# A product-key expert layer on one core: the split of the expert scores between streamed and gathered columns, 1536 and 512 against 1408 and 640

## The chip, the cores and the metric

The kernel runs on one core of one Trainium2 chip. The metric is the device time of one execution, in microseconds (us). The shown time is the median of 3 runs. One more execution was taken by the hardware profiler; its span is the time from its first to its last instruction.

## The reference, cut to what matters

A decoder layer for 256 tokens of 2048 values: a mixer (projections, two convolutions, a recurrence) and then a product-key expert layer. The change is in the expert layer:

```python
q = (hf @ wq).reshape(t, 8, 2, 128)                      # 8 heads, two halves
scores = einsum('thpd,hpnd->thpn', q, subkeys)           # 128 keys per half
# top 16 of each half, then the top 16 of their sums: 16 experts a head and token
expert_idx = row * 128 + col                             # of 16384 experts
act = einsum('cd,chkd->chk', hb, take(u_table, expert_idx))  # the expert scores
w = gates * gelu(act)
y = einsum('chk,chkd->cd', w, take(v_table, expert_idx))
```

Each token needs 128 scores: the products of its 2048 values with the 2048 values of 128 rows of the u table.

## The kernel before, in words

The stages follow one another: modulation and mixer (to about 475 us of the span), queries, top-k and expert scores (about 475 to 1138 us, the stage of the change), the weighting of the chosen experts (about 1138 to 1318 us), the v table and the output.

**The score of one expert is made in two parts.** The first `DU` = 1536 of the 2048 values are streamed: for each of 128 rows of 128 experts (`urows`, 64 to 127 and then 0 to 63) the block `ud[r]` is loaded and multiplied with all 256 tokens on TensorE, and the result goes to row r of the large tile S (L815). The last `GU` = 512 values are gathered: for each of the 256 pairs of a token half (128 tokens, one in each partition) and a chosen slot, GpSimd issues an indirect DMA that brings one row of `ug` per partition (L726), and VectorE forms the product with the tokens' values, which lie in PSUM as `h2n`, and sums it into `actg` (L732, called a dot here). The next stage adds the two parts.

**A streamed row is worked in pieces.** `UPARTS` cuts the `KU` = 12 slices of 128 values into two pieces of 6. `piece` loads its part (L785), splits it on ScalarE into a high part (L95) and on VectorE into a low part (L96, called a sub here), and issues 3 matmuls of 128x256 for each slice (L788, L790 for the high part, L792 for the low one). High and low parts have rings of two buffers each, so a piece can't be split before the piece two ahead of it has left TensorE. The query columns (`wq`, 16 slices in `QPARTS` of 6, 6 and 4) go through the same `piece`; head 0 computes four columns, for heads 0 and 1, head 1 none, each later head two. Four PSUM accumulators (`paccB`) are there beside two banks for `h2n` and one for `misc`.

**The order on VectorE is written out by a planner at build time.** The stage stands in a `manual_schedule` of VectorE. After each piece `room` calls `fill`, which keeps two ledgers in nanoseconds. `clock[1]` is VectorE's free time: each piece adds 327 per slice less the price of its sub, and each top-k step and dot issued takes its price off (`dve(n)` = 69 + n/0.96). `clock[2]` is the DMA's free time: each piece adds 327 per slice less 182 for its own load, capped at the price of one gather, and a gather (`GU`*512/360: 728) is issued while it is above 0, a buffer is free and a chosen slot is known. A dot may come `LAG` = 3 pieces behind its gather. Head h+1 begins after 16 pieces (`NU`); what is left of older top-k work then is issued at once (`finish`).

**The buffers of the gathers** are 6 in the tile R (`guS`) and 30 that are lent from rows of S that aren't written yet (`lend`, rows 12 to 46 and 102 to 128, `UG` = 2 rows each). `retire` takes them back before S is written there, so that in the last 32 streamed rows only those in R are left. R is also where the next stage keeps its transposed indices (`trs`, L882 to L892) and its first two broadcast rows (`rawR`, L949).

**The end of the stage** is this loop; nothing else follows it on VectorE before the next stage:

```python
        while dots or units:
            clock[2] = 1e9
            gathers()
            dot()
```

The next stage (L949 to L999) builds one-hot matrices from `cold` (SyncE load, ScalarE L951 and L952), forms scores in PSUM (L959), picks with VectorE (L965, `choose`), and builds weights with GpSimd (L988, `sides`), VectorE (L993) and TensorE (L995). Its PSUM tiles lie where `h2n` and the accumulators were.

Of the kernel before, what the change touches and what calls it, by code (L numbers as in the profile page):

```python
# [16 lines left out]
AF = mybir.ActivationFunctionType  # L17
# [4 lines left out]
T = 256  # L22
D = 2048
KT = D // 128
# [13 lines left out]
LAG = 3  # L38
DOTS = 3
SLACK = 0  # L40
UG = 2
EG = 2
COLR = 48
BURST = 1
# [2 lines left out]
QPARTS = ((0, 6), (6, 12), (12, 16))  # L47
# [15 lines left out]
XUF = 4  # L63
# [2 lines left out]
MSTEP = (1, 0)  # L66
NFIRST = 10
NACC = 5
DU = 1536
KU = DU // 128  # L70
GU = D - DU
KSL = (6, 6, 4)
DV = 1536
GV = D - DV
UPARTS = ((0, 6), (6, 12))

PCOLS = {}
_n = 0
# [9 lines left out]
def build(nc, tc, A, stop=None):  # L88
# [5 lines left out]
    def split(h, l, src, eng=None):  # L94
        nc.scalar.activation(h, src, AF.Copy)  # L95
        (eng or nc.vector).tensor_tensor(l, src, h, op=OP.subtract)  # L96
# [143 lines left out]
    accum = lambda: pacc.tile([128, T], F32, name="acc")  # L240
# [147 lines left out]
    for j in range(4):  # L388
        n = 0
# [224 lines left out]
    Sf = S.rearrange("p b t r -> p (b t r)")  # L614
# [3 lines left out]

    def flat(a, n):

        return Sf[:, a * T:(a + n) * T]

    def rows(a, n):
        return flat(a, n).rearrange("p (a b) -> p a b", b=T)


    UW = UPARTS[0][1]
    ua = Area(0, RKB - 9)
# [11 lines left out]
    ufR = Area(RKB - 9, RKB).ring(3, UW * 128)  # L640
    guS = [ua.t(GU) for _ in range(int((ua.end - ua.at) // GU))]
    sub = kc(flat(0, 8))
    qring = Ring([rows(8, 2), rows(10, 2)])
    nc.sync.dma_start(sub, A["sub"])
# [105 lines left out]
    def lend(at):  # L750
        lent[at] = flat(at, UG)[:, :GU]
        free.append(lent[at])
# [21 lines left out]
    def finish():  # L774
        for t in tops.pop(0)[1]:
            clock[1] -= t
        gathers()

    def piece(ps, src, k0, k1, end, late=False):

        n = (k1 - k0) * 128
        w = kc(ufR()[:, :n])
        uh, ul = uHr(), uLr()
        with tc.high_priority(offset=HP):
            nc.sync.dma_start(w, src[:, k0:k1, :])  # L785
            split(uh[:, :k1 - k0], ul[:, :k1 - k0], w)
        for k in range(k0, k1):
            nc.tensor.matmul(ps, uh[:, k - k0, :], hH(k), start=k == 0, stop=False)  # L788
            if not late:
                nc.tensor.matmul(ps, uh[:, k - k0, :], hL(k), start=False, stop=False)  # L790
        for k in range(k0, k1):
            nc.tensor.matmul(ps, ul[:, k - k0, :], hH(k), start=False, stop=k == end - 1)  # L792
        for k in range(k0, k1 if late else k0):
            nc.tensor.matmul(ps, uh[:, k - k0, :], hL(k), start=False, stop=False)

    def room(k0, k1):
        n = (k1 - k0) * 128
        fill((k1 - k0) * 327 - dve(n) + SLACK, n * 512 / 360, (k1 - k0) * 327)
# [4 lines left out]
    def upiece():  # L803
        if "parts" not in state or not state["parts"]:
            state["r"] = r = urows.pop(0)
            state["parts"] = list(UPARTS)
            state["ps"] = accum()
# [7 lines left out]
            nc.scalar.activation(srow(r), ps, AF.Copy)  # L815
        room(k0, k1)

    for at in list(range(12, 60 - 3 * XUF - UG, UG)) + list(range(102, 129 - UG, UG)):
        lend(at)
    more = [flat(60 - 3 * i - 3, 3) for i in range(XUF)]  # L820
    with tc.manual_schedule(engines={mybir.EngineType.DVE}):
        for h in range(NH):
            if h != 1:
                n = 4 if h == 0 else 2
                cols = [accum() for _ in range(n)]
                for k0, k1 in QPARTS:
                    for a in range(n):
                        piece(cols[a], A["wq"][2 * h + a], k0, k1, KT, h == 0 and k0 == 0)
                        room(k0, k1)
                qss = [qring() for _ in range(n // 2)]  # L830
                for a in range(n):
                    nc.scalar.activation(qss[a // 2][:, a % 2, :], cols[a], AF.Copy)
            qs = qss.pop(0)
            if h == 0:
                nc.scalar.activation(tab, qs[:, 0, :1], AF.Exp, scale=0.0)
            if h == 0:
                ufR.aps = ufR.aps + more
            for tt in range(2):
                ps = misc()
                for a in range(2):  # L840
                    nc.tensor.matmul(ps[:, 128 * a:128 * a + 128], qs[:, a, tt * 128:tt * 128 + 128],
                                     sub[:, 2 * h + a, :], start=True, stop=True)
                while len(tops) >= 2:
                    finish()
                sc = scR()
                nc.scalar.activation(sc, ps[:, :256].rearrange("p (a b) -> p a b", a=2), AF.Copy)
                tops.append((clock[0], topk(h, tt, sc)))
            for _ in range(NU):
                upiece()
        while tops:  # L850
            upiece()
# [91 lines left out]
    at = lambda g: (g * TG // NK, g * TG % NK)  # L943
# [223 lines left out]
def arrays(i):  # L1167
# [5 lines left out]
    def slabs(w):  # L1173
# [12 lines left out]
        "sub": c_(i["peer_subkeys"][0].reshape(2 * NH, NK, 128).transpose(2, 0, 1)),  # L1186
        "ud": c_(i["peer_u"][0][:, :DU].reshape(NK, NK, KU, 128).transpose(0, 3, 2, 1)),
        "ug": c_(i["peer_u"][0][:, DU:]),
        "vd": c_(i["peer_v"][0][:, :DV].reshape(NK, NK, DV)),
# [13 lines left out]
```

## Time and profile before

| | us |
|---|---|
| median of 3 runs | 1884.22 (1877.45 to 1885.96) |
| the profiled execution, its own time | 1884.01 |
| span of the profiled execution | 1882.0 |
| busy in the span: TensorE matmul | 1795.1 (95%) |
| VectorE | 1523.8 (81%) |
| ScalarE | 958.5 (51%) |
| GpSimd | 786.7 (42%) |
| DMA moved | 530.03 MB, mean 282 GB/s |

In the profile PE is TensorE (PEld its weight loads), DVE is VectorE, ACT is ScalarE, POOL is GpSimd, SP is SyncE. L726 is line 726 of the kernel. `out<-in` are the program's tile names with their digits left out. A busy share is a mean over stages with different limits; what counts is which engine had no gap in the stage in question. Matmuls overlap in the records: one lasts 0.28 us there, while a new one starts every 0.12 us.

### The profile page before, as it was taken

What the parts mean: (1) busy time and instruction counts of PE and PEld (TensorE: products, weight loads), DVE (VectorE), ACT (ScalarE), POOL (GpSimd) and SP (SyncE); (2) the same over time, 40 slices, a digit from 0 to 9 for tenths busy, and PEclk for the clock granted to TensorE, in tenths of its full rate; (3) what the DMA queues carried; (4) which work ended last, traced back from release to release, by engine and by line L of the source; (5) the groups of instructions that cost most, each with busy time, mean ns of one, the idle gap of its engine ahead of it and who ended that gap; (6) DMA issues with size and microseconds to landing.
All of it is one profiled execution on the core that took longest, in us unless ns stands there. A gap on an engine that the chain in (4) does not pass through costs nothing.

```text
span 1882.0 us, 34335 instructions
## 1 busy us (share of the span) xinstructions
PE 1795.1 (95%) x11978; PEld 1544.5 (82%) x11978; DVE 1523.8 (81%) x3946; ACT 958.5 (51%) x1474; POOL 786.7 (42%) x789
## 2 busy tenths in 40 slices
PE   6999999999899999999999998998999999999996
PEld 2667777787899999999999997887777787778774
DVE  3349998755789999999877777999788888888887
ACT  3243333743665555555555558884444444544443
POOL 0000000000035555324555635997776566666662
PEclk8999999999999999999999999999999999999998
DMA  8998889796779989878999886552799889898884
GB/s 311 372 358 277 295 301 322 254 332 249 258 248 302 297 298 300 277 248 288 306 306 305 283 294 200 177 146 80 276 317 335 322 318 313 310 313 313 311 299 155
DMA packets 174652, 530.03 MB, mean 282 GB/s; under 512 B 20736, under 2 KB 44304, under 8 KB 167056
## 3 DMA queue, kind: packets, MB, share of 16 engines
q1 hardware_dynamic: 132656, 391.50, 61.9%
q0 software_dynamic: 40960, 134.25, 19.9%
q8 instruction: 94, 1.54, 0.3%
q10 hardware_dynamic: 864, 2.10, 0.3%
q14 instruction: 78, 0.64, 0.1%
HBM read 521.40 MB, written 6.37 MB: 280 GB/s over the span
## 4 chain that ended last, share of the span: by engine, by line
PE 51%; issue 15%; POOL 14%; DVE 10%; DMA 9%; ACT 2%; SPq 0%; POOLq 0%; ACTq 0%; DVEq 0%
PE acc L788 11%; PE acc L790 11%; PE acc L792 11%; POOL S L1065 7%; DMA PF<-in_w_in_dram 4%; PE acc L354 3%; PE acc L355 3%; PE acc L357 3%; POOL sh L988 3%; PE modps L279 2%; DMA R<-in_vd_dram 2%; POOL sl L1065 2%; POOL sh L1065 2%; PE acc L365 1%; DVE PF L435 1%
## 5 line engine op out<-in xcount | busy, mean ns | idle before, releaser
L788 PE MATMUL acc<-sh,sb 128*128 128x256 f32 x1792 | 443.1, 284 | 1.0 <-ACT sb L95 0.5
L790 PE MATMUL acc<-sl,sb 128*128 128x256 f32 x1768 | 438.9, 284 | 0.4 <-DVE sl L563 0.4
L788 PEld LDWEIGHTS acc<-sh,sb 128*128 128x128 f32 x1792 | 342.6, 192 | 3.4 <-ACT sh L557 2.2
L790 PEld LDWEIGHTS acc<-sl,sb 128*128 128x128 f32 x1768 | 339.3, 192 | 0.6 <-DVE sl L563 0.6
L95 ACT ACTIVATE sb<-R 128x768 fp32r<-128x768 f32 (+2 forms) x203 | 197.1, 971 | 230.0 <-PE acc L790 113.1
L96 DVE TENSOR_TENSOR sb<-S,sb 128x768 fp32r<-128x768 f32 (+3 forms) x274 | 219.0, 800 | 97.0 <-ACT sb L95 84.0
L726 POOL DMA_INDIRECT R<-in_ug_dram,ei x119 | 130.7, 1099 | 386.2 <-ACT gt L705 253.3
L95 ACT ACTIVATE sb<-S 128x768 fp32r<-128x768 f32 (+3 forms) x274 | 207.3, 758 | 115.3 <-PE acc L790 89.4
L792 PE MATMUL acc<-sh,sb 128*128 128x256 f32 x1792 | 264.8, 283 | 0.0
L1065 POOL DMA_INDIRECT S<-in_vg_dram,ei x158 | 214.7, 1359 | 115.6 <-DVE R L1074 84.5
L792 PEld LDWEIGHTS acc<-sh,sb 128*128 128x128 f32 x1792 | 237.1, 192 | 0.0
L1092 PE MATMUL o<-sl,sb 128*128 128x512 f32 x900 | 222.5, 394 | 12.1 <-DVE sl L96 9.4
L1092 PE MATMUL o<-sh,sb 128*128 128x512 f32 x888 | 218.4, 394 | 11.5 <-DVE sh L96 10.2
L726 POOL DMA_INDIRECT S<-in_ug_dram,ei x137 | 153.4, 1120 | 167.4 <-DVE ei L714 97.1
L1092 PEld LDWEIGHTS o<-sl,sb 128*128 128x128 f32 x900 | 166.4, 188 | 57.2 <-DVE sl L96 18.9
L1092 PEld LDWEIGHTS o<-sh,sb 128*128 128x128 f32 x888 | 166.2, 189 | 54.0 <-DVE sh L96 17.8
L96 DVE TENSOR_TENSOR sb<-R,sb 128x768 fp32r<-128x768 f32 (+1 forms) x160 | 150.1, 938 | 51.9 <-ACT sb L95 40.2
L988 POOL TENSOR_SCALAR sh<-iot,R 128x128 f32<-128x128 f32 x248 | 144.8, 602 | 35.3 <-ACT R L892 21.1
L1092 PE MATMUL o<-sb 128*128 128x512 f32 x516 | 126.3, 390 | 0.5 <-ACT sb L95 0.5
L1074 DVE SCALAR_TENSOR_TENSOR R<-S,R 128x512 f32<-128x512 f32 x157 | 117.5, 748 | 3.5 <-DMA S<-in_vg_dram,ei 0.7
L95 ACT ACTIVATE PR<-PF 128x1024 fp32r<-128x1024 f32 (+2 forms) x81 | 66.2, 826 | 95.7 <-DMA PF<-in_w_in_dram 57.5
L1092 PEld LDWEIGHTS o<-sb 128*128 128x128 f32 x516 | 96.7, 188 | 21.2 <-ACT sb L95 0.9
(291 smaller groups left out, 3331.7 us busy)
## 6 DMA issues: line engine op xcount, KB each, us to landing
R<-in_vd_dram SPq DMA_DIRECT2D x128, 768.0 KB
PF<-in_w_mod_dram SPq DMA_DIRECT2D x86, 1024.0 KB
R<-in_ud_dram SPq DMA_DIRECT2D x132, 384.0 KB
S<-in_ud_dram SPq DMA_DIRECT2D x124, 384.0 KB
PF<-in_w_in_dram SPq DMA_DIRECT2D x44, 512.0 KB
PF<-in_w_out_dram SPq DMA_DIRECT2D x32, 512.0 KB
PF<-in_w_in_dram SPq DMA_DIRECT2D x40, 256.0 KB
sl<-in_w_mod_dram SPq DMA_DIRECT2D x20, 512.0 KB
```

The costliest lines, as they stand in the source:

```text
L95: nc.scalar.activation(h, src, AF.Copy)
L96: (eng or nc.vector).tensor_tensor(l, src, h, op=OP.subtract)
L354: nc.tensor.matmul(ps, h[:, k - k0, :], rh(k), start=first and k == k0, stop=False)
L355: nc.tensor.matmul(ps, h[:, k - k0, :], rl(k), start=False, stop=False)
L726: nc.gpsimd.indirect_dma_start(out=g, out_offset=None, in_=A["ug"], in_offset=bass.IndirectOffsetOnAxis(ap=ei[:, tt, s_:s_ + 1], axis=0))
L788: nc.tensor.matmul(ps, uh[:, k - k0, :], hH(k), start=k == 0, stop=False)
L790: nc.tensor.matmul(ps, uh[:, k - k0, :], hL(k), start=False, stop=False)
L792: nc.tensor.matmul(ps, ul[:, k - k0, :], hH(k), start=False, stop=k == end - 1)
L988: eng.tensor_scalar(Bt[:, i, :], iot, trs[tt][:, 1, b + i:b + i + 1], None, op0=OP.is_equal)
L1065: nc.gpsimd.indirect_dma_start(out=g, out_offset=None, in_=A["vg"], in_offset=bass.IndirectOffsetOnAxis(ap=ei[:, tt, s_:s_ + 1], axis=0))
L1074: nc.vector.scalar_tensor_tensor(og[:, tt, :], g, wn[:, tt, s_:s_ + 1], og[:, tt, :], op0=OP.mult, op1=OP.add)
L1092: nc.tensor.matmul(out[tt][n], a[:, tt * 128:tt * 128 + 128], b[:, 512 * n:512 * n + 512], start=r == 0 and a is wh and b is vh, stop=r == ...
```

## The change

The streamed part has 1408 values (11 slices, in pieces of 6 and 5) and the gathered part 640. The lent buffers take 2.5 rows of S each, so that 14 and 10 of them fit where 17 and 13 did, and R holds 5 buffers of 640 values where it held 6 of 512. `h2n` takes two banks for each token half, four in all, and three accumulators are left; for these, every head computes its own two query columns, head 0 and head 1 too. The host cuts the u table accordingly.

```diff
-UG = 2
+UG = 2.5
-DU = 1536
+DU = 1408
-UPARTS = ((0, 6), (6, 12))
+UPARTS = ((0, 6), (6, 11))
@@ flat
-        return Sf[:, a * T:(a + n) * T]
+        return Sf[:, int(a * T):int((a + n) * T)]
@@
-    for at in list(range(12, 60 - 3 * XUF - UG, UG)) + list(range(102, 129 - UG, UG)):
-        lend(at)
+    for a, b in ((12, 60 - 3 * XUF), (102, 128)):
+        for i in range(int((b - a) / UG)):
+            lend(a + i * UG)
@@ for h in range(NH)
-            if h != 1:
-                n = 4 if h == 0 else 2
-                cols = [accum() for _ in range(n)]
-                for k0, k1 in QPARTS:
-                    for a in range(n):
-                        piece(cols[a], A["wq"][2 * h + a], k0, k1, KT, h == 0 and k0 == 0)
-                        room(k0, k1)
-                qss = [qring() for _ in range(n // 2)]
-                for a in range(n):
-                    nc.scalar.activation(qss[a // 2][:, a % 2, :], cols[a], AF.Copy)
-            qs = qss.pop(0)
+            cols = [accum() for _ in range(2)]
+            for k0, k1 in QPARTS:
+                for a in range(2):
+                    piece(cols[a], A["wq"][2 * h + a], k0, k1, KT, h == 0 and k0 == 0)
+                    room(k0, k1)
+            qs = qring()
+            for a in range(2):
+                nc.scalar.activation(qs[:, a, :], cols[a], AF.Copy)
```

`KU`, `GU`, the number of PSUM banks of `h2n` (`HB`), of accumulators (`5 - HB`) and of buffers in R follow from these by the lines of before.

## Rows read from the trace of the kernel before

**Rows 1.** Page: busy us (share of the span) and instructions of each engine.

```profile
PE 1795.1 (95%) x11978; PEld 1544.5 (82%) x11978; DVE 1523.8 (81%) x3946; ACT 958.5 (51%) x1474; POOL 786.7 (42%) x789
```

**Rows 2.** Stretches: from:to length, busy us (instructions) by engine, PEclk, DMA share, GB/s.

```profile
538.00:880.00 342.00, 341.51 (x2827) 339.14 (x2826) 319.25 (x1329) 196.63 (x401) 153.52 (x140) 1.00 0.88 287
880.00:1060.00 180.00, 180.00 (x1503) 180.00 (x1502) 143.30 (x324) 94.12 (x125) 96.28 (x84) 1.00 0.90 296
...
1138.00:1318.00 180.00, 166.03 (x1273) 140.55 (x1272) 164.11 (x822) 131.42 (x231) 149.72 (x252) 0.98 0.51 151
```

**Rows 3.** TensorE at the stage's start, in order of time: start us, duration us, what.

```profile
488.70 0.39 PE L790 MATMUL acc<-sl,sb 128*128 128x256 f32 x1 [0.39 <-DVE sl L563]
...
505.43 0.61 PE L841 MATMUL misc<-S 128*128 128x128 f32 x4
```

**Rows 4.** VectorE at the same place, in order of time: the last low part.

```profile
493.27 0.69 DVE L563 TENSOR_TENSOR sl<-PF,sh 128x512 fp32r<-128x512 f32 x1 [0.36 <-ACT sh L557]
```

**Rows 5.** Source line 726, the gathers: ns min/median/max, first and last start us.

```profile
L726 POOL DMA_INDIRECT S<-in_ug_dram,ei x137: 940/947/1693, 548.2 to 983.9; - x137
L726 POOL DMA_INDIRECT R<-in_ug_dram,ei x119: 940/947/1692, 534.8 to 1118.3; - x119
```

**Rows 6.** Groups by line and shape from 560 to 1240: the subs of two sizes.

```profile
L96 DVE TENSOR_TENSOR sb<-R,sb 128x768 fp32r<-128x768 f32 x131 | 125.2, 955 | 39.5 <-ACT sb L95 31.3 <-issue 7.0 <-ACT R L846 0.8
...
L96 DVE TENSOR_TENSOR sb<-S,sb 128x512 fp32r<-128x512 f32 x6 | 4.2, 695 | 0.3 <-ACT sb L95 0.3
```

**Rows 7.** VectorE in order of time: two dots, one behind the other.

```profile
705.79 0.68 DVE L732 SCALAR_TENSOR_TENSOR R<-S,h2n 128x512 bf16<-128x512 f32 x1
...
706.51 0.69 DVE L732 SCALAR_TENSOR_TENSOR R<-S,h2n 128x512 bf16<-128x512 f32 x1
```

**Rows 8.** Sub, dot and gather in the last streamed rows, in order of time.

```profile
1097.04 0.96 DVE L96 TENSOR_TENSOR sb<-R,sb 128x768 fp32r<-128x768 f32 x1 [0.60 <-ACT sb L95]
...
1097.92 0.68 DVE L732 SCALAR_TENSOR_TENSOR R<-R,h2n 128x512 bf16<-128x512 f32 x1
...
1098.88 0.94 POOL L726 DMA_INDIRECT R<-in_ug_dram,ei  x1 [1.22 <-DVE R L732]
```

**Rows 9.** GpSimd in order of time: two gathers in a row; one during a sub.

```profile
542.10 0.94 POOL L726 DMA_INDIRECT R<-in_ug_dram,ei  x1 [1.57 <-DVE ei L714]
543.34 0.94 POOL L726 DMA_INDIRECT R<-in_ug_dram,ei  x1 [0.30 <-issue]
...
1027.92 0.96 DVE L96 TENSOR_TENSOR sb<-R,sb 128x768 fp32r<-128x768 f32 x1 [0.53 <-issue]
...
1028.31 1.38 POOL L726 DMA_INDIRECT R<-in_ug_dram,ei  x1 [0.30 <-issue]
```

**Rows 10.** The v table's gathers: issue on GpSimd, use on VectorE, two pairs.

```profile
1321.35 1.34 POOL L1065 DMA_INDIRECT sh<-in_vg_dram,ei  x1 [9.81 <-DVE R L1072]
1323.00 2.15 POOL L1065 DMA_INDIRECT sh<-in_vg_dram,ei  x1 [0.31 <-DVE R L1074]
...
1325.60 0.75 DVE L1074 SCALAR_TENSOR_TENSOR R<-sh,R 128x512 f32<-128x512 f32 x1
1329.34 0.75 DVE L1074 SCALAR_TENSOR_TENSOR R<-sh,R 128x512 f32<-128x512 f32 x1 [2.99 <-DMA sh<-in_vg_dram,ei]
```

**Rows 11.** The stage's end, in order of time, VectorE and TensorE.

```profile
1133.76 0.96 DVE L96 TENSOR_TENSOR sb<-R,sb 128x768 fp32r<-128x768 f32 x1 [1.20 <-ACT sb L95]
1137.00 0.88 PE L792 MATMUL acc<-sh,sb 128*128 128x256 f32 x6
...
1140.27 0.35 DVE L965 SCALAR_TENSOR_TENSOR R<-iot,R,G 128x128 bf16<-128x128 f32 x1 [5.55 <-ACT R L892]
1147.60 0.35 DVE L965 SCALAR_TENSOR_TENSOR R<-iot,R,G 128x128 bf16<-128x128 f32 x1 [4.17 <-PE G L959]
1153.42 0.98 PE L995 MATMUL W<-sl,sh 128*128 128x128 f32 x4 [0.80 <-DVE sl L993]
```

**Rows 12.** The chain that ended last, in order of time: start us, us, what.

```profile
1131.41 5.13 DMA R<-cold
```

## The prediction

> **What bounds the kernel now.** I read the page's engine shares first, then the stretches of the stage, then the instructions at its two ends in order of time. The shares put TensorE at 95% [rows 1], which says little about one stage; the stretches say more. From 538 to 1060 us TensorE has no gap (341.51 of 342, 180.00 of 180) [rows 2]; the reader should see that 1503 matmuls in 180 us are one every 0.120 us, and 180/1503 = 0.1198 is the price used below. VectorE is close behind where the top-k work runs (319 of 342, 93%) and loose later (143 of 180); the DMA engines stand at 0.90 with 296 GB/s [rows 2]. So TensorE bounds this stage, with VectorE and the DMA near. In the stage behind it VectorE (164 of 180) and GpSimd (150 of 180) set the pace [rows 2], and TensorE has room.
>
> **The change part by part.**
>
> *The removed slice.* 128 streamed rows lose 3 matmuls each: 384 x 0.1198 = 46.0 us less on the bounding engine. This has one answer as long as nothing else becomes late.
>
> *Two query columns first instead of four.* Before, the four columns give TensorE 4 x 16 x 3 x 0.1198 = 23.0 us of work while the normed tokens are still being made; the last low part comes at 493.27 + 0.69 = 493.96 [rows 4], TensorE waits only in specks such as 0.39 us for a low part [rows 3], and the four columns end at 505.43. Two columns' worth stood 11.5 us earlier, at 493.9. Now the two columns can't end before that low part: 4 slices of the first column use it and the second column's last piece follows (1.4 us), so they end at 495 to 498. VectorE has two subs less to do meanwhile and may bring the low part 1.7 us sooner. The loss is between 0 and 5 us; I take 3.0, from the end of the low part plus the last pieces less a part of those subs. The rings of two forbid that streamed rows come in ahead.
>
> *Pieces of VectorE.* A sub of 768 lasts 955 ns, of 512 695 [rows 6], 1.02 ns an element; its pitch is 1097.92 - 1097.04 = 0.88 us [rows 8], so a sub of 640 has about 0.75. A dot's pitch is 706.51 - 705.79 = 0.72 us [rows 7]; 128 more elements at the sub's slope make 0.85. The planner fills the free time of a 5-slice piece (5 x 327 - 736 = 899 ns) with 899/736 = 1.22 dots: 0.75 + 1.22 x 0.85 = 1.79 us beside 5 x 0.36 = 1.80 on TensorE; a 6-slice piece comes to 0.88 + 1093/736 x 0.85 = 2.14 beside 2.16. VectorE stays just under. For the bursts of left-over top-k work at a head's start, which grow, I take 0.5 us, with 0 and 4 as bounds (a gain is excluded: no matmul waits for VectorE in the long stretches now).
>
> *Three accumulators.* A row is copied out in one ScalarE instruction while the next row takes 4 us, so two would do; nothing.
>
> *The ledger of gathers.* This decides. A gather's price in the ledger rises from 728 to 640 x 512/360 = 910, while a streamed piece credits 6 x 145 = 870 or, with 5 slices, 725. Before, every piece pays for a gather (870 against a cap of 728). Now two pieces give 1595, 1.75 gathers a row. I worked the planner's rules through piece by piece. For before this gives 137 gathers into S and 119 into R, as the trace has [rows 5], and none left at the end. For after: the first gather at the 21st piece instead of the 26th; 75 issued by row 101; then no buffer is free in 74 of the 91 pieces to row 10 (38 pieces before), because there are 29 larger buffers instead of 36 and VectorE's ledger can't pay the dots sooner; 127 by row 12; 217 at the last piece. **39 gathers and 41 dots remain for the closing loop**, where nothing streams any more.
>
> *The price of that loop.* Each gather needs one of the 5 buffers of R. GpSimd's pitch is 543.34 - 542.10 = 1.24 us, 0.94 busy and 0.30 of issue [rows 9]. The loop of a buffer is the dot 0.85, then GpSimd's start 1098.88 - 1097.92 - 0.72 = 0.24 behind it [rows 8], 0.94, and the landing. No row shows the landing of a ug gather alone; the v table's bound it: in the first pair of [rows 10] at most 1325.60 - 1322.69 = 2.9 us (no wait is shown), in the second 1329.34 - 1325.15 = 4.2 (VectorE waits, under full DMA load). I take 3.2, near the first, since little else is loaded then. 0.85 + 0.24 + 0.94 + 3.2 = 5.2 us over 5 buffers is 1.05 a gather, so GpSimd's 1.24 paces, and with 4.2 still (6.2/5 = 1.25). Where it begins: the last sub starts 1137.88 - 1133.76 = 4.1 us before TensorE's end [rows 11], now 0.36 less, 3.7; sub, dot and 0.24 later, 1.9 us before the end, GpSimd starts. The last dot is done at -1.9 + 38 x 1.24 + 0.94 + 3.2 + 0.85 = 50.2 us behind TensorE's end. VectorE's order puts the next stage behind these dots, and that stage's PSUM tiles lie where `h2n` is, so all of it is exposed: +50.2. Bounds: 48, and 67 if every gather lasts 1.38 as one does that starts in a sub [rows 9] (38 x 1.68).
>
> The Trainium skill (SBUF — State Buffer, "SBUF: two separate sides") gives the reason that would decide between these: VectorE and GpSimd share a port pair by an exclusive lock, and a GpSimd-issued DMA can't write its descriptors while VectorE runs an operation of the locking kind. The gather of 1.38 agrees: 1028.31 + 1.38 is 0.9 us behind the sub's end near 1028.8. By its condition (two SBUF inputs, or a two-port mode) the dot, with one input in PSUM, would not lock and the sum stays; if it did, rival 2 below is the result.
>
> *The restart.* Before, the next stage starts badly: first pick at 1140.27, then 4.17 us of waiting, first weights at 1153.42 [rows 11], 15.5 us behind TensorE's end; without the wait and from the first pick it takes 9.0. Its second set of loads was waiting for TensorE's buffers and is now there early. But the first broadcast rows lie on the third last gather's buffer: released 2.5 us before the last dot, then a load of 5.13 us [rows 12] and some 2 us of ScalarE and TensorE. So the first pick comes about 4.7 us behind the last dot, the weights at 13.7: a gain of 1.8 us, between -1 and 7.
>
> **Sum**: -46.0 + 3.0 + 0.5 + 50.2 - 1.8 = +5.9 us. The profiled execution took 1884.0 (span 1882.0), 0.2 from the median: 1890. The bounds of all terms together reach from -46.0 + 48 - 7 = -5 (1879) to -46.0 + 5 + 4 + 67 + 1 = +31 (1915).
>
> **The rivals.**
> 1. *The loop is hidden* (faster). If the next stage's one-hots and scores ran beside the closing gathers, or the gathers were out by the end as now, only -46.0 + 3.5 would be left: 1841.5. Against it: the 39, whose count rests on rules that reproduce the trace, and the shared PSUM. 0.06.
> 2. *GpSimd is held by the dots, or rows of 2560 bytes cost it more*: 1.68 a gather, 67 instead of 50 us: 1907. For it: some gathers last to 1.69 [rows 5]; against it: these start in subs, which the loop has not. 0.17.
> 3. *DMA.* While gathers run, a row needs 0.721 MB + 1.75 x 0.328 = 1.29 MB in 3.95 us, 327 GB/s. At 296 for a share of 0.90 [rows 2] the ceiling is 329. If the loads only keep 312, a row takes 4.14, and 60 rows lose 11 us: 1901. It decides from 4.5% below the needed rate. 0.17.
> 4. *VectorE becomes the pace* in the stretch that is at 93% [rows 2]: 0.1 us in each of some 170 pieces, which its 0.02 of slack allows: +17, 1907. 0.08.
>
> That the change does nothing would need TensorE not to bound; [rows 2] excludes it.
>
> **How the numbers follow.** Forecast 0.52, rivals 0.06, 0.17, 0.17, 0.08. The measurement can tell 0.5% (9.4 us) from no change. The forecast's own range is 1882 to 1897, so 0.48 of its 0.52 within 0.5% and 0.04 slower; rival 2 slower but for 0.02, rival 3 but for 0.04, rival 4 but for 0.01. Faster 0.06, same 0.55, slower 0.39. The range reaches from the lower bound of the terms past rivals 2 to 4, 1879 to 1908; what lies above needs several bad terms at once.
>
> **What would show it.** Right: 384 matmuls fewer in the stage at the same 0.12 us; a stretch of some 50 us behind the last L792 with 39 L726 at 1.24 us, 41 L732 of about 0.81 us, and TensorE idle; S and R gathers at 110 and 146. Wrong: matmuls waiting for subs or loads in the long stretch (rivals 3, 4), gathers of 1.4 us in the loop (rival 2), or picks (L965) beside gathers (rival 1).

## The result, and the profile after

The changed kernel takes 1897.08 us (median, 1893.97 to 1901.02) against 1884.22: a ratio of 1.0080, with a 95% interval of 1.0061 to 1.0098. It is slower by 0.8%, more than the 0.5% that can be told from no change. The profiled execution took 1897.37, its span is 1895.3, 13.3 longer than before; the sums below are of spans. From the changed lines on, line numbers are two smaller than before (L841 is L839, L965 is L963, L995 is L993).

The page's engine shares, busy us and share of the span, answer [rows 1]:

```profile
PE 1756.2 (93%) x11596; PEld 1502.8 (79%) x11596; DVE 1539.8 (81%) x3946; ACT 944.0 (50%) x1474; POOL 765.1 (40%) x789
```

The 382 matmuls fewer are the 384 that were removed (two records are missing). They took 38.9 us of busy time with them, and yet the time rose. The stretches show where (from:to, length, busy us and instructions of TensorE, its weight loads, VectorE, ScalarE and GpSimd, granted clock, DMA share, GB/s); they answer [rows 2]:

```profile
538.00:880.00 342.00, 341.56 (x2825) 338.93 (x2824) 318.79 (x1290) 200.01 (x417) 118.59 (x116) 1.00 0.87 292
880.00:1060.00 180.00, 179.66 (x1497) 179.38 (x1496) 152.58 (x343) 97.18 (x137) 83.99 (x82) 1.00 0.93 323
1060.00:1099.00 39.00, 39.00 (x328) 39.00 (x327) 31.39 (x59) 19.79 (x28) 21.05 (x19) 1.00 0.92 316
1099.00:1153.00 54.00, 0.83 (x5) 0.36 (x3) 33.25 (x82) 5.37 (x9) 34.93 (x37) 0.52 0.88 284
```

Down to 1099 us nothing is new: TensorE is full at the same 0.120 us a matmul. The last row is what wasn't there before: 54 us in which TensorE does nothing, while GpSimd issues 37 gathers and VectorE makes their dots. The source lines of the gathers (ns min/median/max, first and last start) and TensorE's first instruction after the stage (the bracket is the idle time before it, and what ended it) say the same:

```profile
L726 POOL DMA_INDIRECT R<-in_ug_dram,ei x146: 940/946/1752, 529.8 to 1147.4; - x146
L726 POOL DMA_INDIRECT S<-in_ug_dram,ei x110: 940/946/1884, 537.9 to 955.8; - x110
...
1152.51 0.45 PE L889 MATMUL misc<-ident,R 128*128 128x128 f32 x1 [53.12 <-DVE R L881]
```

The counts are 110 into S and 146 into R, where [rows 5] had 137 and 119, and the last gather starts 48 us behind TensorE's end. That end and the last dot, from TensorE and VectorE in order of time (start us, duration us):

```profile
1098.63 0.76 PE L792 MATMUL acc<-sh,sb 128*128 128x256 f32 x5
...
1151.38 0.81 DVE L732 SCALAR_TENSOR_TENSOR R<-R,h2n 128x640 bf16<-128x640 f32 x1
```

**The account.** I call TensorE's end in the stage P (1098.63 + 0.76 = 1099.39; before 1137.88 [rows 11]) and the end of the last dot D (1151.38 + 0.81 = 1152.19). P came 38.5 us earlier, D is 52.8 behind P, and from D to the end of the span there are 743.1 us, where before there were 744.1 from P. -38.5 + 52.8 - 1.0 = +13.3, the whole difference of the spans.

Of the 38.5, 2.4 lie ahead of the stage: the square root that opens the norm (L575) started at 465.20 against 467.63. This start lies between 461.7 and 467.6 in the profiled executions of all the kernels below, so stages are compared from this point on, and it is called t0. The two rows, before and after:

```profile
467.63 0.51 ACT L575 ACTIVATE R<-R,epsc 128x256 f32<-128x256 f32 x1 [4.05 <-DVE R L573]
...
465.20 0.51 ACT L575 ACTIVATE R<-R,epsc 128x256 f32<-128x256 f32 x1 [4.05 <-DVE R L573]
```

From t0 to P it took 670.25 us before and 634.19 after: 36.1 us of the 46.0 that were removed. So 9.9 us were lost within the stage, nearly all at its start, as TensorE's rows there show (they answer [rows 3]):

```profile
474.46 1.93 PE L279 MATMUL modps<-PF,cs 128*32 128x512 f32 x8 [1.63 <-DMA PF<-in_w_mod_dram]
478.41 1.11 PE L288 MATMUL misc<-ident,R 128*128 128x128 f32 x4 [2.02 <-ACT R L285]
481.65 0.47 PE L611 MATMUL h2n<-ident,PF 128*128 128x128 f32 x1 [2.13 <-ACT PF L556]
483.04 1.65 PE L788 MATMUL acc<-sh,sb 128*128 128x256 f32 x6 [0.92 <-DVE modc L289]
...
501.17 0.46 PE L839 MATMUL misc<-S 128*128 128x128 f32 x2 [2.22 <-DMA R<-in_ud_dram]
```

The first matmul of a query column starts 17.8 us behind t0, and the scores of head 0 wait 2.2 us for a load. Before, that first matmul started 7.0 us behind t0:

```profile
474.66 0.98 PE L788 MATMUL acc<-sh,sb 128*128 128x256 f32 x6 [0.41 <-ACT sh L557]
```

To compare kernels that differ in order, I take t0 to the first streamed row's copy (L815) and subtract the matmuls done by then at 3 x 0.1198 us a slice. The copies, ScalarE in order of time, before, after, and of two experiments below (in this order):

```profile
510.42 0.66 ACT L815 ACTIVATE S<-acc 128x256 f32<-128x256 f32 x1
...
505.14 0.66 ACT L815 ACTIVATE S<-acc 128x256 f32<-128x256 f32 x1
...
514.00 0.64 ACT L815 ACTIVATE S<-acc 128x256 f32<-128x256 f32 x1
...
509.31 0.64 ACT L815 ACTIVATE S<-acc 128x256 f32<-128x256 f32 x1
```

| kernel | t0 | first copy | slices by then | not filled with matmuls |
|---|---|---|---|---|
| before | 467.63 | 510.42 | 64 + 12 | 42.8 - 27.3 = 15.5 |
| after | 465.20 | 505.14 | 32 + 11 | 39.9 - 15.5 = 24.5 |
| banks in another order | 466.66 | 504.60 | 32 + 11 | 37.9 - 15.5 = 22.5 |
| before, 360 ns a slice | 461.69 | 507.53 | 64 + 12 | 45.8 - 27.3 = 18.5 |
| before, two columns first | 461.77 | 500.87 | 32 + 12 | 39.1 - 15.8 = 23.3 |
| columns two and two | 463.92 | 514.00 | 64 + 11 | 50.1 - 27.0 = 23.1 |
| both | 464.06 | 509.31 | 64 + 11 | 45.3 - 27.0 = 18.3 |

Before against after: 9.0 us lost at the start. Not all of it need be the change's, since each row is one execution. The kernel before with 360 ns a slice runs the same start as the kernel before, and its execution still lost 3.0 more (18.5): TensorE's granted clock was at 0.50, its lower level of 1.2 GHz, from 465 to 470 us and again from 499 to 501, which it never is at the start of the kernel before, and two waits at the first scores were 0.9 us longer. Seven of the kernels here run the start of the changed kernel; their executions lost 23.7 to 26.7, the two highest with a second fall of the clock. Two groups of matmuls of the kernel before with 360, on either side of the first fall, and its stretch from 465 to 470 us:

```profile
461.70 1.06 PE L279 MATMUL modps<-PF,cs 128*32 128x512 f32 x8 [1.00 <-DMA PF<-in_w_mod_dram]
465.42 1.94 PE L279 MATMUL modps<-PF,cs 128*32 128x512 f32 x8 [2.65 <-DMA PF<-in_w_mod_dram]
...
465.00:470.00 5.00, 3.65 (x16) 0.40 (x16) 4.90 (x7) 3.37 (x6) 0.00 (x0) 0.50 1.01 398
```

The changed kernel's matmuls of 1.93 us at 474.46 are of the same kind. Against the execution with the low clock, then, 6.0 of the 9.0 us come with the order of the columns (5.2 to 8.2 over the seven executions), and 3.0 are a difference between executions, most of it beside the low clock.

### The profile page after: what moved, and what is told of

It is laid out like the page before. It is cut to its first block, busy times and chain, and to the rows that moved or that the text cites. A ratio compares the mean times of both kernels' runs of the same rounds, so it can differ in the third digit from the quotient of the medians.

```text
span 1895.3 us, 33602 instructions
## 1 busy us (share of the span) xinstructions
PE 1756.2 (93%) x11596; PEld 1502.8 (79%) x11596; DVE 1539.8 (81%) x3946; ACT 944.0 (50%) x1474; POOL 765.1 (40%) x789
## 4 chain that ended last, share of the span: by engine, by line
PE 38%; issue 21%; POOL 19%; DMA 11%; DVE 10%; ACT 1%; POOLq 0%; SPq 0%; ACTq 0%; DVEq 0%
POOL S L1063 7%; PE acc L788 6%; PE acc L792 6%; PE acc L790 6%; POOL R L726 4%; DMA PF<-in_w_in_dram 4%; POOL sh L986 3%; PE acc L354 3%; PE acc L355 3%; PE acc L357 3%; DMA R<-in_ug_dram,ei 2%; PE modps L279 2%; POOL sh L1063 2%; POOL sl L1063 2%; PE acc L365 2%
## 5 line engine op out<-in xcount | busy, mean ns | idle before, releaser
L788 PE MATMUL acc<-sh,sb 128*128 128x256 f32 x1664 | 414.5, 285 | 0.9 <-DVE modc L289 0.9
L790 PE MATMUL acc<-sl,sb 128*128 128x256 f32 x1652 | 410.0, 283 | 0.0
L788 PEld LDWEIGHTS acc<-sh,sb 128*128 128x128 f32 x1664 | 319.2, 192 | 1.3 <-DVE modc L289 1.2
L790 PEld LDWEIGHTS acc<-sl,sb 128*128 128x128 f32 x1652 | 317.1, 192 | 0.0
L95 ACT ACTIVATE sb<-R 128x640 fp32r<-128x640 f32 (+3 forms) x200 | 187.8, 939 | 221.7 <-PE acc L790 100.9
L96 DVE TENSOR_TENSOR sb<-S,sb 128x256 fp32r<-128x256 f32 (+3 forms) x277 | 212.8, 770 | 87.9 <-ACT sb L95 86.6
L95 ACT ACTIVATE sb<-S 128x256 fp32r<-128x256 f32 (+3 forms) x277 | 203.3, 735 | 117.6 <-PE acc L790 91.3
L792 PE MATMUL acc<-sh,sb 128*128 128x256 f32 x1664 | 250.4, 284 | 0.3 <-DVE sb L96 0.3
L792 PEld LDWEIGHTS acc<-sh,sb 128*128 128x128 f32 x1664 | 222.2, 192 | 0.5 <-DVE sb L96 0.5
L1090 PEld LDWEIGHTS o<-sh,sb 128*128 128x128 f32 x888 | 166.6, 190 | 54.5 <-DVE sh L96 18.5
L726 POOL DMA_INDIRECT S<-in_ug_dram,ei x110 | 113.2, 1030 | 200.5 <-DVE ei L714 97.3
L96 DVE TENSOR_TENSOR sb<-R,sb 128x768 fp32r<-128x768 f32 (+2 forms) x157 | 138.9, 885 | 38.1 <-ACT sb L95 30.5
L732 DVE SCALAR_TENSOR_TENSOR R<-R,h2n 128x640 bf16<-128x640 f32 x146 | 119.1, 816 | 26.1 <-DMA R<-in_ug_dram,ei 25.4
```

Source lines behind the costliest of these rows:

```text
L726: nc.gpsimd.indirect_dma_start(out=g, out_offset=None, in_=A["ug"], in_offset=bass.IndirectOffsetOnAxis(ap=ei[:, tt, s_:s_ + 1], axis=0))
L732: nc.vector.scalar_tensor_tensor(gjR(), g, 1.0, h2n[:, tt, :GU], op0=OP.mult, op1=OP.mult, accum_out=actg[:, tt, s_:s_ + 1])
L1090: nc.tensor.matmul(out[tt][n], a[:, tt * 128:tt * 128 + 128], b[:, 512 * n:512 * n + 512], start=r == 0 and a is wh and b is vh, stop=r == ...
```

## The experiments

All are run beside the kernel before. In short:

| kernel | gathers left for the loop | median us | ratio to before, 95% |
|---|---|---|---|
| changed | 39 | 1897.1 | 1.0061 to 1.0098 |
| changed, PSUM pools in another order | 39 | 1900.2 | 1.0064 to 1.0097 |
| before, two columns first | 0 | 1891.4 | 1.0026 to 1.0056 |
| changed, closing loop left out | 0 | 1842.2 | 0.9767 to 0.9806 |
| changed, 360 ns a slice | 0 | 1856.9 | 0.9842 to 0.9877 |
| before, 360 ns a slice | 0 | 1891.3 | 1.0029 to 1.0068 |
| changed, gather's price 728 | 25 | 1878.0 | 0.9973 to 1.0009 |
| changed, gather's price 1200 | 67 | 1938.9 | 1.0259 to 1.0330 |
| the last, four more buffers | 67 | 1938.0 | 1.0274 to 1.0338 |
| changed, columns two and two | 40 | 1901.6 | 1.0077 to 1.0131 |
| changed, two and two, 355 ns | 1 | 1855.2 | 0.9817 to 0.9883 |
| changed, 355 ns | 0 | 1847.6 | 0.9795 to 0.9850 |
| changed, two and two, banks, 358 ns | 0 | 1844.4 | 0.9788 to 0.9840 |

### The start: is it the banks, or the order of the columns?

Two kernels take the two readings apart. The first keeps the change and lets the accumulators lie in other PSUM banks, so that the first column needn't wait for the bank of the modulation step:

```diff
-    ph2 = psB.enter_context(pool("ph2", space=PSUM))
-    pacc = psB.enter_context(pool("paccB", 5 - HB, space=PSUM))
     pmisc = psB.enter_context(pool("pmiscB", 1, space=PSUM))
+    pacc = psB.enter_context(pool("paccB", 5 - HB, space=PSUM))
+    ph2 = psB.enter_context(pool("ph2", space=PSUM))
```

> The changed kernel with the three PSUM pools of the stage taken in another order: misc, then the three accumulators, then the four banks of h2n, so that the accumulators lie on banks that are free early. Theory A (the late first query column, 483.0 instead of 474.7 us, comes from an accumulator on a bank that the modulation's last transposes hold until 482.8): the first L788 starts at 472 to 476 and TensorE leaves the stage 4 to 7 us earlier, 1889 to 1894 us. Rival B (it comes from having two query columns instead of four): the first L788 may be early, but the streamed rows begin when they do now and the time stays at 1895 to 1899.

The second is the kernel before with only the order of the columns changed (the hunk at L824 of the diff):

> The kernel before with one part of the change alone: two query columns for each head, in place of four for head 0 and none for head 1. Streamed and gathered columns, banks and buffers as before. Theory A: the columns cost only what the prediction said, 2 to 5 us at the start, and gathers all end in the stage: 1885 to 1890 us. Rival B (the columns' order is what delays the start by 8 us): 1890 to 1894.

The banks alone gain nothing: 1900.19 us, though the first column now starts 7.6 us behind t0. The order of the columns alone costs 7.1 us (1891.44 against 1884.32 beside it), more than twice the 3.0 of my sum. In its trace TensorE starts early and then stops when the two columns are done:

```profile
480.76 0.51 PE L788 MATMUL acc<-sh,sb 128*128 128x256 f32 x2 [0.61 <-ACT sh L557]
...
493.57 0.58 PE L788 MATMUL acc<-sh,sb 128*128 128x256 f32 x1 [2.98 <-ACT sb L95]
```

At 493.57 TensorE waits for the next piece's split on ScalarE. That split stands behind the two column copies, which wait for TensorE, and behind the table load:

```profile
491.29 1.28 ACT L832 ACT_TABLE_LOAD   x1
...
492.69 0.83 ACT L95 ACTIVATE sb<-S 128x768 fp32r<-128x768 f32 x1
```

With four columns other matmuls stood there. So it is the missing work, not the bank, that costs at first; whether the bank costs once the work is there was open, and two later kernels tell.

### The loop: what it costs, and what leaves the gathers over

The first of these leaves out the gathers and dots of the closing loop (39 and all but the two already in flight), so that these scores lack their gathered part:

```diff
-        while dots or units:
-            clock[2] = 1e9
-            gathers()
+        units.clear()
+        while dots:
             dot()
```

> The changed kernel without its closing gathers: the 39 that are left when the streamed rows end are neither gathered nor multiplied, so 39 of 256 slots keep no gathered part. Theory A (the loop stands alone behind TensorE's end): 39 x 1.25 us less, 1845 to 1851 us. Rival B (half of it is covered by work of the next stage, and the loss is elsewhere): 1865 to 1880.

1842.17 us, 54.9 less. The idle 53 us are the loop's, and without it the change would be worth 42 us. Its trace also shows how far one execution can be trusted: up to P it runs what the changed kernel runs, but from t0 to P it took 638.9 us (634.2), and from the next stage's first weights to the end 717.7 (728.1), where nothing was changed. In the fourteen executions the latter time lies between 717.7 and 731.9.

The second keeps all work and pays VectorE's and the DMA's ledgers 360 ns a slice in place of 327, in `room`:

```diff
-        fill((k1 - k0) * 327 - dve(n) + SLACK, n * 512 / 360, (k1 - k0) * 327)
+        fill((k1 - k0) * 360 - dve(n) + SLACK, n * 512 / 360, (k1 - k0) * 360)
```

> The changed kernel with 360 ns a slice in both ledgers of the planner in place of 327, near the measured 359. By the planner's rules no gather is left for the closing loop. Theory A (TensorE still bounds the stage): 1845 to 1853 us, gathers of R and S all before the last L792. Rival B (VectorE, which is now given 10% more in each piece, is over full in the top-k stretch, matmuls wait for subs): 1855 to 1880. Rival C (DMA: 193 MB in 617 us is 313 GB/s in the mean and the loads come late): L788 waits for loads, 1855 to 1880.

1856.91 us: 142 gathers go into S, 114 into R, the last of them starts at 1088.7 us, and there is no loop. 40 of the 55 us come back. Most of the rest is lost before P, much of it in the stretch in which the top-k work runs. From 600 to 780 us, the changed kernel and then the one with 360:

```profile
600.00:780.00 180.00, 179.56 (x1485) 178.00 (x1484) 167.32 (x701) 104.86 (x225) 60.12 (x59) 1.00 0.85 285
...
600.00:780.00 180.00, 178.94 (x1455) 175.49 (x1454) 178.97 (x742) 105.91 (x223) 79.85 (x79) 1.00 0.92 316
```

VectorE is busy for 178.97 of 180 us, and TensorE issues 30 matmuls fewer, 3.6 us of work, though its busy share hardly falls: short waits don't show in it, the count does. It is 21 lower from 505 to 600 us, too, and 63 lower from 780 to 940, together 114 matmuls or 13.7 us; what those 63 wait for I have not followed. From t0 to P this kernel takes 651.9 against 634.2.

The same edit in the kernel before is the control:

> The kernel before with 360 ns a slice in place of 327 in both ledgers; nothing else. It has no closing loop to lose. Theory A, that the 40 us which 360 brought to the changed kernel are the closing loop alone, expects nothing gained: 1884 to 1896, since matmuls will wait for subs as they did with 360 in the changed kernel (about 4 to 13 us). Rival B, that the larger ledger is better in itself (fewer bursts at the heads' starts), expects a time below 1880, and then only a part of the 40 us is the loop's.

1891.25 us, 0.49% slower. A larger ledger is no gain in itself; what it brings to the changed kernel is the loop.

**The price of a gather left over.** Two kernels move the ledger's price of a gather, and with it only the count that is left: 728 and 1200 in place of 910 (also as the cap).

```diff
-            clock[2] -= GU * 512 / 360
+            clock[2] -= 1200
...
-        clock[2] = min(clock[2] + (pe - load) * DMAF, BURST * GU * 512 / 360)
+        clock[2] = min(clock[2] + (pe - load) * DMAF, BURST * 1200)
```

> The changed kernel with 1200 in place of 910 as a gather's price in the ledger of gathers (and as its cap). By the planner's rules 67 gathers and 69 dots are left for the closing loop in place of 39 and 41. Theory A, that the loop costs GpSimd's pitch for each gather left, expects 28 x 1.25 = +35 us: 1932. Rival B, that a good part of the loop's price is its beginning (the landing waits of 1100 to 1115 us) and the restart, expects less than 1.25 for each, at VectorE's pitch of 0.85: +24, 1921. Rival C, that the DMA stays the bound in the loop, expects more, 1.4 or over: +40, 1937 or over.

> The changed kernel with the price of a gather of 512 values, 728, in place of 910 in the ledger of gathers (and as its cap); VectorE's ledger stays at 327. By the planner's rules 25 gathers and 28 dots are left for the closing loop in place of 39 and 41. Theory A, that each gather left costs GpSimd's pitch and that the price was only a part of the cause, since VectorE's ledger still can't pay the dots, expects 14 x 1.25 = 17.5 us less than the changed kernel: 1880. Rival B, that most of the 55 us is a fixed cost of the loop (its first landings, the cold clock, the restart), expects 1885 to 1895. Rival C, that cheaper gathers overload the DMA and the streamed rows come late, expects no gain or a loss: 1895 to 1905, with matmuls that wait for loads.

TensorE's idle time at the end, for 25 and for 67 gathers left (39: 53.12):

```profile
1134.52 0.45 PE L889 MATMUL misc<-ident,R 128*128 128x128 f32 x1 [36.88 <-DVE R L881]
...
1196.29 0.45 PE L889 MATMUL misc<-ident,R 128*128 128x128 f32 x1 [90.84 <-DVE R L881]
```

14 gathers fewer take 16.2 us of it, 1.16 each. The time, 1877.97, is theory A's within 2 us; it is 19.1 below the changed kernel's, but the kernel before was 3.4 us faster beside it (1880.86), and against that the gain is 15.8, 1.13 each. The price was only a part of the cause: at the old price 25 of the 39 are still left, while 360 ns a slice leaves none. That edit raises both ledgers, and no run raises one alone; the planner's rules, which give the counts of all these kernels, leave 25 with 360 in the ledger of gathers alone and 6 with 360 in VectorE's alone. By the rules, VectorE's ledger is the larger part. 28 gathers more take 37.7 us, 1.35 each, and 41.8 us of the time, 1.49 each. That is more than GpSimd's 1.25, the number of rival C, but not by its cause: the DMA share in this loop is 0.73 to 0.89 from 1120 to 1190 us.

A candidate for the 1.35 is that five buffers turn round too slowly. The kernel with 1200 was given four more in the loop:

```diff
+        free.extend(v[:, :GU] for v in ufR.aps)
         while dots or units:
```

> The kernel with 1200 as a gather's price (67 gathers and 69 dots in the closing loop, 1938.9), and in that loop four more buffers for the gathers, the ones into which the streamed rows were loaded: nine in place of five. Theory A, that five buffers turn round too slowly (dot 0.9, start 0.25, gather 0.95, landing of 4 to 5 us, divided by 5) where GpSimd's own pitch is 1.25, expects the 1.46 us that each of the added 28 gathers cost to fall to 1.25: 93 us of loop become about 83 to 86, 1929 to 1932. Rival B, that the landings are long because the DMA engines are full, expects them to grow with more gathers in flight and the time to stay: 1936 to 1940.

1938.02 us, no gain; theory A fell, and its rival too in its reason, since the DMA isn't full here either (0.63 to 0.85 from 1140 to 1190 us). The trace splits the loop. From 1112 to 1148 us GpSimd keeps its own pitch without a break (29 gathers, one every 1.25 us), and up to the gather of 1132.22 the dots start 3 to 4 us behind the end of theirs. Behind it the dots fall back further and further, until no buffer is free at 1149 us in spite of the nine. GpSimd and VectorE in order of time (the dots' brackets are the waits), and the stretch from 1140 to 1150 us in the columns of the stretches above:

```profile
1133.47 0.95 POOL L726 DMA_INDIRECT R<-in_ug_dram,ei  x1 [0.30 <-issue]
1134.72 0.95 POOL L726 DMA_INDIRECT R<-in_ug_dram,ei  x1 [0.30 <-issue]
...
1138.92 0.82 DVE L732 SCALAR_TENSOR_TENSOR R<-R,h2n 128x640 bf16<-128x640 f32 x1 [1.62 <-remote]
1141.71 0.82 DVE L732 SCALAR_TENSOR_TENSOR R<-R,h2n 128x640 bf16<-128x640 f32 x1 [1.96 <-remote]
1144.51 0.82 DVE L732 SCALAR_TENSOR_TENSOR R<-R,h2n 128x640 bf16<-128x640 f32 x1 [1.97 <-issue]
...
1140.00:1150.00 10.00, 0.00 (x0) 0.00 (x0) 3.08 (x7) 0.00 (x0) 6.69 (x8) 0.50 0.83 262
```

The dots come 2.80 us apart where gathers go out every 1.25. The data isn't what is late: 262 GB/s is a gather's 0.328 MB every 1.25 us, and in the trace's DMA packets the last one of each gather ends 2.2 to 2.9 us behind GpSimd from 1133 to 1186 us, while the dots start up to 9.6 us behind it. So the landings don't grow, though rival B expected it; VectorE takes the data up late. The profile puts these waits down to "remote" and "issue", and what holds VectorE is open. With five buffers the same begins 53 us behind P, and the changed kernel's own loop shows none of it up to its last gather, 48 us behind P.

### Putting the start right

In the changed kernel, the columns of heads 0 and 1 are computed before head 0's scores again, but two and then two, for which three accumulators do:

```diff
-            cols = [accum() for _ in range(2)]
-            for k0, k1 in QPARTS:
-                for a in range(2):
-                    piece(cols[a], A["wq"][2 * h + a], k0, k1, KT, h == 0 and k0 == 0)
-                    room(k0, k1)
-            qs = qring()
-            for a in range(2):
-                nc.scalar.activation(qs[:, a, :], cols[a], AF.Copy)
+            for b in (range(2) if h == 0 else range(1, 2) if h > 1 else ()):
+                hb = h + b if h == 0 else h
+                cols = [accum() for _ in range(2)]
+                for k0, k1 in QPARTS:
+                    for a in range(2):
+                        piece(cols[a], A["wq"][2 * hb + a], k0, k1, KT, hb == 0 and k0 == 0)
+                        room(k0, k1)
+                qss.append(qring())
+                for a in range(2):
+                    nc.scalar.activation(qss[-1][:, a, :], cols[a], AF.Copy)
+            qs = qss.pop(0)
```

> The changed kernel with the columns of heads 0 and 1 computed before head 0's scores, as before the change, but two and then two, so that three accumulators do; the ledger is as in the changed kernel and leaves 40 gathers and 43 dots to the closing loop (39 and 41). Theory A, that the missing 4 to 6 us at the stage's start are the cover that the second pair gave to the load of the keys, the column copies and ScalarE's table load behind the first, expects 1890 to 1893 (less 5 to 8, plus 1.3 for the loop), and no matmul of L839 that waits over 1 us for a load. Rival B, that the loss comes from the chain ahead of the first matmul, which has only two columns' work beside it either way, expects no gain: 1897 to 1900.

1901.64 us, no gain. The waits of L839 for the load are gone, as theory A had it, but the start lost hardly less (23.1 against 24.5 in the table above, and 23.7 to 26.7 in all executions of that start), and the first column still came 17.8 us behind t0; matmuls now waited 4.0 us for subs at the heads' starts (0.3 in the changed kernel). With the larger ledger added:

> The changed kernel with both: columns of heads 0 and 1 two and two ahead of head 0's scores, and 355 ns a slice in both ledgers, by which 1 gather and 4 dots are left at the end. Theory A, that the changed kernel holds 46 us less of TensorE's work and gives it back only in the loop and at the start, expects 1845 to 1850. Rival B, that a larger ledger makes VectorE late wherever it empties the queue of gathers, expects 1854 to 1860, as with 360 alone.

1855.22 us: rival B's number. But not by its reason: P lies 639.2 us behind t0, as in the kernel without the loop (638.9). From P to the end it took 751.7 us, where the kernel without the loop took 733.4. One gather and four dots in the loop hold the next stage back: the last dot waits 2.54 us for its landing and ends 4.8 us behind P, and the first weights come 19.8 us behind P, 4.1 later than without the loop (15.7). The other 14 of the 18 us lie behind the first weights, 731.9 us to the end against 717.7, the two ends of the spread named above.

Then the order two and two together with the other banks (and 358 ns, by which no gather and one dot are left):

> The changed kernel with three edits that bear on the stage's start and on the loop: the columns of heads 0 and 1 two and two ahead of head 0's scores, the PSUM pools in the order misc, accumulators, h2n (so that the first columns don't wait for the bank of the modulation step), and 358 ns a slice in both ledgers (1 dot left at the end). Theory A, that the two causes at the start hide one another (alone, neither edit gained), expects the first streamed row copied out at 43 to 46 us behind the square root that opens the norm (before 42.8, with the pairs alone 50.1), and 1843 to 1850 in all. Rival B, that two accumulating columns can't cover the norm however they are placed, expects that row at 48 to 50 and 1852 to 1857.

The first streamed row is copied 45.3 us behind t0, where theory A had 43 to 46, and the time is 1844.36 us. In the table above the banks gain 2.0 us alone, the pairs 1.4, the two together 6.2 of the 9.0. The first two are no more than executions of one start differ by (23.7 to 26.7, with the pairs 23.1 and 23.7); 18.3 lies well below all of them, so in this execution each cause hid the other. 18.3 us not filled are what the kernel before with 360 ns has (18.5), which also ran its first microseconds at the low clock; by that measure all that the order cost is back.

And the ledger alone, with 355:

> The changed kernel with 355 ns a slice in place of 327 in both ledgers; nothing else. By the planner's rules no gather and no dot is left for the end (the last gather stands at streamed row 61, with 360 at row 58). Theory A, that the whole of the loop's 55 us comes back and that VectorE is late a little less often than with 360, expects 1846 to 1853. Rival B, that VectorE is as late as with 360 or that the last gathers' landings stand in the way, expects 1855 to 1860.

1847.64 us, theory A: 49.4 of the loop's 54.9 us are back, and the matmuls of 600 to 780 us are 1464, between 1455 with 360 and 1485 with 327. Both kernels beat the one before by 1.8%, and their intervals overlap; I don't rank them.

## Why the prediction came out as it did

The range of 1879 to 1908 holds 1897.08, and the direction of the sum, +5.9, is right; measured were +12.9 of the medians. But the likeliest class was "within 0.5%" and it is slower by 0.8%, so the likeliest number, 1890, is 7 us short, and the forecast's own range of 1882 to 1897 is just missed. The wider range had been stretched for rivals 2 to 4, none of which came; that it holds the time is in part luck. Step by step:

- **The removed slice, -46.0.** Right: 0.120 us a matmul, and 384 of them.
- **Two query columns first, +3.0 with bounds 0 to 5.** This is the mis-sized term: 9.0 in the trace, 6.0 of it against the execution with the low clock (and 7.1 when the order alone was changed). I bounded it by the last low part and the pieces behind it, as if TensorE would be done with the rest by then. The low part came at 492.04, but TensorE, which had begun at 483.04, had 44 of its 96 column matmuls still to do. They ended at 497.5, within the 495 to 498 of the step, but 32.3 us behind t0 where two columns' worth stood at 26.3 before: 6.0 lost; the other 3.0 lie behind the columns. Three things were not in the step. The accumulators lie in the modulation step's bank, and hold the first column until 17.8 us behind t0. Behind the columns nothing covers ScalarE's queue and the load of the keys (2.2 us at 501.17), which the other two columns did before. And the clock at 0.50 makes the first six matmuls 1.65 us for 0.98, which no step can foresee from one execution. A term for moved work has to ask what that work was covering.
- **Pieces of VectorE, +0.5.** About right: matmuls wait 0.3 us for a sub in the whole stage, and some 0.9 us are lost in specks. Rival 4 didn't come.
- **Three accumulators, nothing.** Right.
- **The ledger of gathers.** Right to the piece: 110 and 146, as worked out from the rules. That the price alone wasn't the cause but also the ledger of VectorE with the fewer buffers was in the step; that 728 leaves 25 and 360 ns none agrees, though 360 raises both ledgers.
- **The loop, +50.2.** 52.8 measured. Its parts moved more than the sum. The pitch is 1.25 (predicted 1.24), and from 1122 us on a landing takes 3.0 to 3.5 us (predicted 3.2 from an estimate between 2.9 and 4.2). The first ones are longer, because streamed rows and the next stage's loads are still in flight: share 1.03 and 355 GB/s from 1100 to 1110 us. These are the loop's first ten microseconds:

```profile
1102.70 0.94 POOL L726 DMA_INDIRECT R<-in_ug_dram,ei  x1 [0.30 <-issue]
1103.34 0.82 DVE L732 SCALAR_TENSOR_TENSOR R<-R,h2n 128x640 bf16<-128x640 f32 x1 [2.31 <-DMA R<-in_ug_dram,ei]
1104.43 0.94 POOL L726 DMA_INDIRECT R<-in_ug_dram,ei  x1 [0.80 <-DVE R L732]
1106.57 0.82 DVE L732 SCALAR_TENSOR_TENSOR R<-R,h2n 128x640 bf16<-128x640 f32 x1 [2.40 <-DMA R<-in_ug_dram,ei]
...
1107.66 0.94 POOL L726 DMA_INDIRECT R<-in_ug_dram,ei  x1 [2.29 <-DMA R<-in_ug_dram,ei]
```

  The dot of 1106.57 is that of the gather of 1098.95, whose landing took 6.7 us. With 6 us of landing, five buffers, not GpSimd, pace the loop. From the first gather of the loop to the last it took 53.8 us, 6.3 more than 38 x 1.25, nearly all before 1116 us: about 3.4 by these landings, the rest beside VectorE's last subs, where buffers come free late and a gather lasts 1.49. Against it, the loop's first gather starts 5.8 us ahead of P, not 1.9, since GpSimd isn't in VectorE's order. That the two misses largely cancel is luck.
- **The restart, -1.8.** -1.0. The first weights come 1167.19 - 1152.19 = 15.0 us behind the last dot, 13.7 was predicted, 15.5 before [rows 11]; the first pick 6.0, not 4.7. The load of the first broadcast rows is issued at 1149.99, and ScalarE takes them up at 1153.06.

Together: 5.9 + 6.0 (start) + 2.6 (loop) + 0.8 (restart) + 0.4 (specks) - 2.4 (the earlier t0) = 13.3.

**The rivals.** Rival 1 (the loop hidden, 1841.5) is nearly what the kernel without the loop takes, 1842.2; its mechanism was excluded rightly. Rival 2 (1.68 us a gather) is out: 27 gathers that start beside nothing but dots, from 1115 to 1150 us (count, busy us, mean ns, idle before and its releasers):

```profile
L726 POOL DMA_INDIRECT R<-in_ug_dram,ei x27 | 25.5, 945 | 9.2 <-DVE R L732 5.3 <-issue 3.7 <-DMA R<-in_ug_dram,ei 0.3
```

A gather that starts in a sub still takes longer:

```profile
1091.68 0.82 DVE L96 TENSOR_TENSOR sb<-R,sb 128x640 fp32r<-128x640 f32 x1
1091.83 1.49 POOL L726 DMA_INDIRECT R<-in_ug_dram,ei  x1 [1.34 <-DVE R L732]
```

It ends at 1093.32, 0.82 behind the sub. The Trainium skill (SBUF — State Buffer, "SBUF: two separate sides") counts an operation with two SBUF inputs among those that take the port pair shared with GpSimd, though only against a GpSimd operation that reads SBUF. Both rows agree with it, if the gather, which takes its indices from `ei` in SBUF, counts as one.

Rival 3 (the DMA at a ceiling of 329) is out: from 880 to 1060 us TensorE ran 179.66 of 180 at 323 GB/s. How far the ceiling was off shows in the kernel with 355, from 940 to 1000 us, TensorE full:

```profile
940.00:1000.00 60.00, 60.00 (x503) 60.00 (x501) 50.40 (x108) 32.10 (x45) 32.64 (x32) 1.00 0.98 356
```

I had scaled 296 GB/s at a share of 0.90 up to a share of 1; but 356 pass at 0.98, so the busy share is no linear measure of what is left.

## What to carry to other kernels

A smaller bound on one engine is worth only what the planner behind it lets through: count, by its rules, what is left over when the bounding engine is done, price each item by the slowest link of its loop, and give the planner's prices a second look whenever a tile gets larger; here 355 ns in place of 327 turned +0.8% into -1.8%. Of work that is moved away from a stage's start, ask what it was covering (in-order queues, loads, PSUM banks), not only when it could end. And where two causes hide one another, undoing either alone shows nothing, so try both. And know how far executions of the same code differ (here 5 us in this stage, 14 in those behind it) before a microsecond is put down to a cause.

## What the runs showed of the hardware that was not expected

- Landings of a gather of 128 rows of 2560 bytes took 3.0 to 3.5 us with the DMA at a share of 0.85, and 5.7 to 6.7 us at a share of 0.99 to 1.03 (the gathers of 1098.95 to 1104.43).
- In loops of 67 gathers VectorE fell behind late in the loop (dots 2.80, then 1.40 us apart, at gathers 1.25 apart), with five buffers and with nine, though the last packet of each gather still came 2.2 to 3.2 us behind GpSimd's end. The cause is open.
- Ahead of the stage, where TensorE waits for the modulation weights (2.65 us before the row of 465.42 above), the granted clock fell from 1.00 to 0.50 (1.2 GHz) in thirteen of the fourteen profiled executions, and not in that of the kernel before: eight matmuls of 128x512 took 1.94 us for 1.06. Two executions of one start differed by 3.0 us beside this.
